# Attention keys with four rows of a column side by side, and one sum of bias and mask for the two middle query tiles

## The chip, the cores and the metric

The kernel runs on one core of one Trainium2 chip. The metric is the time of one execution in microseconds on the device. The kernel before was timed three times: 905.06, 905.87 and 906.93 us, so its median is 905.87 us.

A core has five engines with a queue of instructions each: PE (matrix products; the load of its weights is listed apart as PEld), DVE (vector), ACT (activations), POOL (general) and SP (here only DMA issue). Each engine works its queue in order. [...]

## The reference

One layer over 1024 latent tokens (a grid of 16 rows and 64 columns) and 256 context tokens, width 1024. One input projection feeds two branches, whose outputs are gated, joined and sent through one output projection.

```python
def hybrid_layer(...):
    h = rmsnorm(x, g_pre) * (1.0 + scale[:, None]) + shift[:, None]
    na_q, na_k, na_v, na_z, g_qkv, g_z, g_b, g_a = jnp.split(h @ w_in, IN_SPLITS, axis=-1)
    o_na = neighborhood_attention(heads(na_q), heads(na_k), heads(na_v), heads(na_kc), heads(na_vc), rpb)
    q, k, v = gdn_qkv(g_qkv, conv_w)
    q, k = axial_rope(q, rope), axial_rope(k, rope)
    beta, g = gdn_gates(g_b, g_a, A_log, dt_bias)
    o_g, o_gc = bidirectional_gdn(q, k, v, g, beta, qc, kc, vc, gc, betac)
    o_g = rmsnorm(o_g, gdn_norm_w).reshape(B, L, GDN_W).astype(x.dtype)
    y = jnp.concatenate([o_na * jax.nn.silu(na_z), o_g * jax.nn.silu(g_z)], axis=-1) @ w_out
    x = x + gate[:, None] * rmsnorm(y, g_post)

def neighborhood_attention(q, k, v, k_ctx, v_ctx, rpb):       # row_block, for each grid row r
    rs = jnp.clip(r - kh // 2, 0, rows - kh)                  # kh = 8 rows, NA_KW = 16 columns
    k_win = k_rows[:, :, col_idx]
    bias = rpb[:, row_off[:, None, None], col_off[None, :, :]]
    s_loc = jnp.einsum('bchd,bicjhd->bhcij', q_r, k_win) + bias
    s_ctx = jnp.einsum('bchd,bnhd->bhcn', q_r, k_ctx)
    p = jax.nn.softmax(jnp.concatenate([s_loc, s_ctx], axis=-1), axis=-1)
    return p_loc @ v_win + p_ctx @ v_ctx                      # as einsums

def gated_delta_chunked(...):                                 # chunk by chunk, one direction
    def step(state, xs):
        v_new = u_n - w_n @ state
        o_n = q_n @ state + qk_n @ v_new
        state = state * gl_n + k_n.T @ v_new
```

There are 8 attention heads of 64 and 4 delta heads of 128; the delta scan runs in both directions.

## The kernel before

**Stages.** Projections, convolution and the preparation of the scan take the first 554 us. Then attention and the delta scan run together (`phase_b`), and the output projection (`phase4`) closes the kernel. Instructions are recorded in program order and then put in an order by a scheduler, which works by a model of the engines and of the buffers; on the chip that order is fixed, engine by engine.

**Keys.** `qk_out` takes a projected tile of queries (i = 0) or keys (i = 1) of a pair of heads from PSUM: ACT writes its rounded part `hi` (L522, tile `sh_k` or `sh_q`), DVE the remainder `lo` (L523, `sl_k` or `sl_q`), and two DMAs bring both to `qk_dram`. gr is 0 or 1 for the 512 latents of 8 grid rows, 2 for the 256 context tokens. Keys of latents lie row by row, 64 columns in a row.

**Attention.** `na_attn` loads a pair of heads p (keys `kk`, queries `qh` and `ql`, bias rows `gt`, values `vv`) and runs 2 × 4 units, rt by ct: rt is the half of the grid, ct the tile of query columns. A unit (`na_unit`) treats 128 queries of 8 rows by 16 columns and both heads hh. Its window is three blocks of four rows with NCOLS = 24, 32, 32, 24 columns for ct = 0 to 3, so n = 288 or 384 keys in three runs of m = 96 or 128. For each head:

- POOL adds bias and mask to `gm` (L676). GCOL0 and CTYPE give the part of the bias and the mask; for ct = 1 and 2 they are the same.
- PE multiplies by the context keys into `pc` (L684) and by the window's keys into `pl` (L688), each with `qh` and `ql`. In L688 the keys are read with the four rows of a column after one another, 64 elements apart.
- DVE takes the largest context score `mi` (L692), and adds `gm` to `pl` and takes the common maximum `nm` (L693); ACT takes the exponentials (L694, L695).
- PE transposes the probabilities into the banks of `pl` and `pc` (L697, L702), DVE and ACT copy them to `tl` and `tcx` (L699, L704), and PE multiplies them with the values into `po` (L710, L715).

After four units DVE gathers the sums, POOL spreads their reciprocals to `rb` (L618), PE transposes these (`prt`, L621), and DVE scales the output `zs` (L623). There are two buffers of `gm` and three of the tiles that hold probabilities.

**Scan.** `delta_scan` runs 4 heads with 10 steps, both directions d in a step. POOL scales `kd` and `vb` (L1125, L1128). Per direction PE, DVE, PE, ACT, PE and DVE follow one another: L1133 into `pa`, `y` (L1134), L1138, `vn` (L1140 or L1142), L1144, the new state `s` (L1147). The output products L1152 and L1153 go to `pos`. The head's output is normed (ACT squares at L1170, POOL L166, L167, L1173; L1175 on POOL or L1179 on DVE), transposed (`ot`, L1182) and gated (L1184). 1.40 steps are recorded for each attention unit.

**Output weights.** After the third pair, and again for the rest in `phase4`, `split_w` loads half a block of `w_out` to `wor` (two buffers), ACT rounds it (L647), POOL takes the remainder (L648). `phase4` multiplies by them in three products each (L1218 to L1220), beginning with the attention output of the last pair, which `split_m` casts (L659, L660).

Of the kernel before, what the change touches and what calls it, by code (L numbers as in the profile page):

```python
# [11 lines left out]
F32 = mybir.dt.float32  # L12
F32R = mybir.dt.float32r
I32 = mybir.dt.int32
AF = mybir.ActivationFunctionType
ALU = mybir.AluOpType
# [4 lines left out]
P = 128  # L21
# [9 lines left out]
KCOL0 = (0, 8, 24, 40)  # L31
# [108 lines left out]
class K:  # L140
    def __init__(self, tc, I, out, dbg=None):
        self.tc, self.nc, self.I, self.out = tc, tc.nc, I, out
        self.dbg = dbg or {}
        self.na_first = None
        self.gate = self.after = None

    def order(self, r, before):
# [369 lines left out]
    def qk_out(self, p, i, gr, src):  # L517
        nc = self.nc
        n, scale, c0 = 512 if gr < 2 else CT, 1.0 if i else 0.125, S * i + 512 * gr
        src, rows = src[:, :n], slice(P * p, P * p + P)  # L520
        hi, lo = (self.wp.tile([P, 512], F32R, name=f"s{c}_{'qk'[i]}{p}{gr}", tag="st", bufs=4)[:, :n] for c in "hl")
        nc.scalar.activation(hi, src, AF.Copy, scale=scale)  # L522
        nc.vector.scalar_tensor_tensor(lo, src, scale, hi.bitcast(F32), ALU.mult, ALU.subtract)  # L523
        nc.sync.dma_start(self.qk_dram[0, rows, c0:c0 + n], hi.bitcast(F32))
        nc.sync.dma_start(self.qk_dram[1, rows, c0:c0 + n], lo.bitcast(F32))

# [136 lines left out]
    def na_unit(self, ps, p, rt, ct, qk, vv, gts, mk, sums, po):  # L663

        nc = self.nc
        u = 4 * rt + ct
        nco = NCOLS[ct]
        n, m = 12 * nco, 4 * nco
        mo = MOFF[(rt, CTYPE[ct])]
        tls, tcs = [], []  # L670
        for hh in range(2):
            gt = gts[hh]
            gv = bass.AP(gt.tensor, gt[:, (4 * (1 - rt)) * 31 + GCOL0[ct]:].offset,
                         [list(gt.ap[0]), [4 * 31, 3], [1, nco], [31, 4]])
            gm = self.nw.tile([P, 384], F32, name=f"gm{p}_{u}_{hh}", tag="gm", bufs=2)
            nc.gpsimd.tensor_tensor(gm[:, :n].rearrange("p (n c r) -> p n c r", c=nco, r=4), gv,  # L676
                                    mk[:, mo:mo + n].rearrange("p (n c r) -> p n c r", c=nco, r=4), ALU.add)
            pcb = ps.tile([P, 512], F32, name=f"pc{p}_{u}_{hh}", tag="sc", bufs=2)
            pl = ps.tile([P, 512], F32, name=f"pl{p}_{u}_{hh}", tag="sl", bufs=2)
            pc = pcb[:, :256]  # L680
            pl3 = pl[:, :n].rearrange("p (n c r) -> p n c r", c=nco, r=4)
            qs, kk = qk[hh]
            for i, a in enumerate(qs):
                nc.tensor.matmul(pc, a[:, u * P:(u + 1) * P], kk[:, S:S + CT], start=(i == 0), stop=(i == 1))  # L684
            kv = kk[:, 256 * rt:256 * rt + 768].rearrange("p (n r c) -> p n c r", c=64, r=4)[
                :, :, KCOL0[ct]:KCOL0[ct] + nco, :]
            for i, a in enumerate(qs):
                nc.tensor.matmul(pl3, a[:, u * P:(u + 1) * P], kv, start=(i == 0), stop=(i == 1))  # L688
            mi = self.nw.tile([P, 1], F32, name=f"mi{p}_{u}_{hh}", tag="mi", bufs=4)
            nm = self.nw.tile([P, 1], F32, name=f"nm{p}_{u}_{hh}", tag="nm", bufs=4)  # L690
            pt = self.nw.tile([P, 640], F32, name=f"pt{p}_{u}_{hh}", tag="pt", bufs=3)
            nc.vector.tensor_reduce(mi, pc, AX.X, ALU.max, negate=True)  # L692
            nc.vector.tensor_tensor_reduce(pt[:, :n], pl[:, :n], gm[:, :n], -1.0, mi, ALU.add, ALU.min, nm)  # L693
            nc.scalar.activation(pt[:, :n], pt[:, :n], AF.Exp, bias=nm, scale=-1.0, accum_out=sums[:, ct, hh, 0:1])  # L694
            nc.scalar.activation(pt[:, 384:640], pc, AF.Exp, bias=nm, accum_out=sums[:, ct, hh, 1:2])  # L695
            for rc in range(3):
                nc.tensor.transpose(pl[:m, rc * P:(rc + 1) * P], pt[:, rc * m:(rc + 1) * m], self.ident)  # L697
            tl = self.nw.tile([P, 384], F32, name=f"tl{p}_{u}_{hh}", tag="tl", bufs=4)
            nc.vector.tensor_copy(tl[:m, :], pl[:m, :384])  # L699
            tls.append(tl)  # L700
            for cc in range(2):
                nc.tensor.transpose(pc[:, cc * P:(cc + 1) * P], pt[:, 384 + cc * P:384 + (cc + 1) * P], self.ident)  # L702
            tcx = self.nw.tile([P, 2, P], F32, name=f"tcx{p}_{u}_{hh}", tag="tcx", bufs=4)
            nc.scalar.copy(tcx.rearrange("p c q -> p (c q)"), pc)  # L704
            tcs.append(tcx)

        for cc in range(2):
            for hh in (1, 0):
                hb = 64 * hh
                nc.tensor.matmul(po[hb:hb + 64, ct, :], self.vcx[:, cc, P * p + hb:P * p + hb + 64], tcs[hh][:, cc, :],  # L710
                                 start=(cc == 0), stop=False, tile_position=(0, hb))
        for rc in range(3):
            for hh in (1, 0):
                hb = 64 * hh
                nc.tensor.matmul(po[hb:hb + 64, ct, :], vv[:m, ct, rt + rc, hb:hb + 64], tls[hh][:m, rc * P:(rc + 1) * P],  # L715
                                 start=False, stop=(rc == 2), tile_position=(0, hb))
# [677 lines left out]
```

## Time and profile before

| | |
|---|---|
| Median of three runs | 905.87 us (905.06 to 906.93) |
| Profiled execution | 904.01 us, of which its span is 902.3 us |
| Mean granted clock of PE in it | 0.963 |
| First score product of attention | 554.23 us |
| First weight product of the output projection | 791.59 us |
| Last product, end of the span | 894.89 us, 902.3 us |
| L676, sums of bias and mask | 64: 32 of 128x288 at 891 ns, 32 of 128x384 at 1127 ns |
| L688, window's scores | 128 products; 288 columns with `qh` 409 ns, 384 columns 455 ns |

A row of a timeline has start and duration in us, the engine, the line, the operation with its output and inputs, the number of instructions, and in brackets the engine's idle time before it with what ended it. A row of groups has the count, then the busy time in us and the mean in ns, then the idle time of the engine before them. A row of the windows has for each engine its busy time with the number of instructions, then the granted clock of PE as a share of full speed, the DMA share and GB/s. A busy PE is modelled: its products overlap, so steps from start to start are the better measure.

### The profile page before, as it was taken

How to read it: one execution, taken by the hardware profiler on the slowest of the kernel's cores; microseconds unless marked ns; L12 is line 12 of the kernel's file. 1: busy time of each engine (PE TensorE's matmuls, PEld its weight loads, DVE VectorE, ACT ScalarE, POOL GpSimd, SP SyncE). 2: the span in 40 equal slices, each digit the busy share in tenths (PEclk: the TensorE clock that was granted, in tenths of full speed). 3: DMA queues.
4: the chain of work that ended last, by engine and by line, in shares of the span. 5: the costliest groups of instructions: out<-in, count | busy, mean ns of one | idle time of the engine just before them, and what ended most of it. 6: DMA issues, size and time to landing. Idle time of an engine off the chain costs nothing.

```text
span 902.3 us, 16602 instructions
## 1 busy us (share of the span) xinstructions
PE 848.5 (94%) x6082; PEld 708.7 (79%) x6082; DVE 537.6 (60%) x1179; ACT 416.2 (46%) x1165; POOL 369.6 (41%) x431
## 2 busy tenths in 40 slices
PE   6999999999999989998998998999999988998996
PEld 4688887887788767787887877888887876887785
DVE  3463454456545699689428634677777775662442
ACT  5262525545645445652334444555545656532310
POOL 1432322614543532455241124568557569423210
PEclk9999999999999989999998985999999998999898
DMA  9786432346355534733799699949387152132351
GB/s 343 257 290 228 150 107 74 114 157 199 89 198 185 138 122 151 216 99 112 249 265 265 219 281 413 267 117 296 141 208 272 48 183 76 47 117 94 108 183 60
DMA packets 95176, 160.98 MB, mean 178 GB/s; under 512 B 28581, under 2 KB 55542, under 8 KB 92918
## 3 DMA queue, kind: packets, MB, share of 16 engines
q1 hardware_dynamic: 87606, 146.25, 51.2%
q10 hardware_dynamic: 7488, 13.67, 4.9%
q8 instruction: 48, 0.79, 0.4%
q14 instruction: 34, 0.28, 0.1%
HBM read 110.82 MB, written 52.42 MB: 181 GB/s over the span
## 4 chain that ended last, share of the span: by engine, by line
PE 64%; DVE 13%; DMA 9%; ACT 5%; issue 4%; POOL 2%; SPq 2%; ACTq 0%; DVEq 0%; POOLq 0%
PE py L1218 3%; PE py L1219 3%; PE py L1220 3%; DVE tb L1003 3%; PE pl L688 2%; DVE vb L1006 2%; PE po L715 2%; PE pl L697 2%; PE pz L464 2%; PE pc L684 2%; PE pz L460 2%; PE pz L465 2%; PE po L710 2%; PE pa L1138 2%; PE pa L1144 2%
## 5 line engine op out<-in xcount | busy, mean ns | idle before, releaser
L676 POOL TENSOR_TENSOR gm<-gt,mk 128x288 f32<-128x288 f32 (+1 forms) x64 | 64.3, 1009 | 36.0 <-DVE nm L693 35.9
L1125 POOL TENSOR_SCALAR kd<-kt,kd 128x128 f32<-128x128 f32 x72 | 43.4, 606 | 35.3 <-PE pa L1144 33.7
L694 ACT ACTIVATE pt<-pt,nm 128x288 f32<-128x288 f32 (+1 forms) x64 | 36.7, 574 | 35.7 <-DVE nm L693 35.5
L945 ACT ACTIVATE em<-em,gc 128x128 f32<-128x128 f32 x80 | 25.5, 391 | 38.2 <-DMA em<-gc_dram 32.3
L693 DVE CUSTOM_DVE_ANT_0 pt<-pl,gm,mi 128x288 f32<-128x288 f32 (+1 forms) x64 | 36.1, 564 | 11.5 <-PE pl L688 4.9
L699 DVE COPY tl<-pl 96x384 f32<-96x384 f32 (+1 forms) x64 | 35.3, 551 | 10.2 <-PE pl L697 9.9
L692 DVE TENSOR_REDUCE mi<-pc 128x1 f32<-128x256 f32 x64 | 26.8, 420 | 22.0 <-PE pc L684 21.1
L464 PE MATMUL pz<-hl,wh_gz 128*128 128x512 f32 x96 | 38.6, 402 | 0.0
L460 PE MATMUL pz<-hh,wh_gz 128*128 128x512 f32 x96 | 38.4, 400 | 0.0
L465 PE MATMUL pz<-hh,wl_gz 128*128 128x512 f32 x96 | 38.3, 399 | 0.0
L473 PE MATMUL pv<-wh_nv,hh 128*128 128x264 f32 x128 | 35.5, 295 | 2.5 <-ACT hh L262 1.7
L964 POOL TENSOR_SCALAR_AFFINE_SELECT qe<-qe 128x256 f32<-128x256 f32 x32 | 26.9, 840 | 25.8 <-DVE qe L963 25.8
L475 PE MATMUL pv<-wl_nv,hh 128*128 128x264 f32 x128 | 35.7, 286 | 1.5 <-POOL wl_nv L446 1.5
L474 PE MATMUL pv<-wh_nv,hl 128*128 128x264 f32 x128 | 36.5, 289 | 0.0
L1003 DVE TENSOR_TENSOR tb<-ab,vb 120x31 f32<-120x31 f32 (+15 forms) x62 | 32.1, 518 | 6.8 <-DMA ab<-ab_dram 5.1
L960 DVE SCALAR_TENSOR_TENSOR pm<-pk,beta,em 128x128 f32<-128x128 f32 x80 | 23.6, 343 | 19.9 <-PE pk L953 12.3
L697 PE MATMUL pl<-c,pt 128*96 128x128 f32 (+1 forms) x192 | 33.7, 285 | 1.4 <-ACT pt L694 1.2
L812 DVE SCALAR_TENSOR_TENSOR acc_v<-xp_v,cols,acc_v 128x1282 f32<-128x1282 f32 x16 | 27.5, 1719 | 9.0 <-ACT acc_v L810 8.9
L1138 PE MATMUL pa<-y,tm 128*128 128x128 f32 x144 | 29.1, 287 | 2.8 <-DVE y L1134 2.2
L1266 ACT ACTIVATE finv<-py 128x512 f32<-128x512 f32 x16 | 9.5, 599 | 46.8 <-PE py L1220 28.3
L1128 POOL TENSOR_SCALAR vb<-v,beta 128x128 f32<-128x128 f32 x40 | 24.2, 606 | 16.7 <-DVE y L1134 10.6
L704 ACT COPY tcx<-pc 128x256 f32<-128x256 f32 x64 | 23.8, 372 | 15.3 <-PE pc L702 15.1
(438 smaller groups left out, 2928.8 us busy)
## 6 DMA issues: line engine op xcount, KB each, us to landing
wada<-in_w_ada SPq DMA_DIRECT2D x16, 512.0 KB, 9.1
em<-gc_dram SPq DMA_DIRECT2D x20, 256.0 KB, 4.6
pm_dram<-pm SPq DMA_DIRECT2D x20, 256.0 KB, 3.3
pmf<-pm_dram SPq DMA_DIRECT2D x8, 640.0 KB, 8.0
tm_dram<-tm SPq DMA_DIRECT2D x8, 640.0 KB, 7.0
kk<-qk_dram SPq DMA_DIRECT2D x16, 320.0 KB, 7.9
tm<-tm_dram SPq DMA_DIRECT2D x4, 1280.0 KB
kq_dram<-kq SPq DMA_DIRECT2D x4, 1152.0 KB
```

The source lines that it names most:

```text
L460: r = nc.tensor.matmul(ps, wh, xh, start=(k == 0), stop=False)
L464: nc.tensor.matmul(ps, wh, xl, start=False, stop=False)
L465: nc.tensor.matmul(ps, wl, xh, start=False, stop=(k == KC - 1))
L474: nc.tensor.matmul(ps, xl, wh, start=False, stop=False)
L475: nc.tensor.matmul(ps, xh, wl, start=False, stop=(k == KC - 1))
L676: nc.gpsimd.tensor_tensor(gm[:, :n].rearrange("p (n c r) -> p n c r", c=nco, r=4), gv, mk[:, mo:mo + n].rearrange("p (n c r) -> p n c r", ...
L693: nc.vector.tensor_tensor_reduce(pt[:, :n], pl[:, :n], gm[:, :n], -1.0, mi, ALU.add, ALU.min, nm)
L694: nc.scalar.activation(pt[:, :n], pt[:, :n], AF.Exp, bias=nm, scale=-1.0, accum_out=sums[:, ct, hh, 0:1])
L697: nc.tensor.transpose(pl[:m, rc * P:(rc + 1) * P], pt[:, rc * m:(rc + 1) * m], self.ident)
L1003: nc.vector.tensor_tensor(t3, bc(ab[:, 0:m, m:m + 1], [r, m, n]), bc(vb[:, m:m + 1, m:], [r, m, n]), ALU.mult)
L1125: nc.gpsimd.tensor_scalar(kd, kt_[:, t, :], self.kd[:, h, d, t:t + 1], None, ALU.mult)
L1138: nc.tensor.matmul(pa, tm[:, d, t, :], y, start=True, stop=True)
```

## The change

Three things are edited. Keys of latents are written in `qk_out` with the four rows of a column side by side: ACT and DVE read the PSUM tile in the order block, column, row, and write SBUF contiguously; for keys, whose scale is 1, DVE's fused operation becomes a plain subtraction. L688's moving operand then is three contiguous runs of m elements. And `gm` is made only for ct = 0, 1 and 3; the unit ct = 2 reads the sum that ct = 1 left, for which there are three buffers instead of two.

```diff
+        self.gm = {}
...
-        nc.scalar.activation(hi, src, AF.Copy, scale=scale)
-        nc.vector.scalar_tensor_tensor(lo, src, scale, hi.bitcast(F32), ALU.mult, ALU.subtract)
+
+        kv = lambda v, o: v.rearrange(f"p (n {o}) -> p n c r", r=4, c=64) if i and gr < 2 else v
+        nc.scalar.activation(kv(hi, "c r"), kv(src, "r c"), AF.Copy, scale=scale)
+        if i:
+            nc.vector.tensor_tensor(kv(lo, "c r"), kv(src, "r c"), kv(hi, "c r").bitcast(F32), ALU.subtract)
+        else:
+            nc.vector.scalar_tensor_tensor(lo, src, scale, hi.bitcast(F32), ALU.mult, ALU.subtract)
...
-            gm = self.nw.tile([P, 384], F32, name=f"gm{p}_{u}_{hh}", tag="gm", bufs=2)
-            nc.gpsimd.tensor_tensor(gm[:, :n].rearrange("p (n c r) -> p n c r", c=nco, r=4), gv,
-                                    mk[:, mo:mo + n].rearrange("p (n c r) -> p n c r", c=nco, r=4), ALU.add)
+
+            if ct != 2:
+                self.gm[hh] = self.nw.tile([P, 384], F32, name=f"gm{p}_{u}_{hh}", tag="gm", bufs=3)
+                nc.gpsimd.tensor_tensor(self.gm[hh][:, :n].rearrange("p (n c r) -> p n c r", c=nco, r=4), gv,
+                                        mk[:, mo:mo + n].rearrange("p (n c r) -> p n c r", c=nco, r=4), ALU.add)
+            gm = self.gm[hh]
...
-            pl3 = pl[:, :n].rearrange("p (n c r) -> p n c r", c=nco, r=4)
+            pl3 = pl[:, :n].rearrange("p (n f) -> p n f", f=m)
...
-            kv = kk[:, 256 * rt:256 * rt + 768].rearrange("p (n r c) -> p n c r", c=64, r=4)[
-                :, :, KCOL0[ct]:KCOL0[ct] + nco, :]
+            kv = kk[:, 256 * rt:256 * rt + 768].rearrange("p (n f) -> p n f", f=256)[
+                :, :, 4 * KCOL0[ct]:4 * KCOL0[ct] + m]
```

The added lines shift what follows: L688 becomes L697, L697 becomes L706, L1138 becomes L1147 and so on, by 6 to 9 lines.

The order on the engines is the same up to the start of attention, and differs from there on. In the rows the numbers after a name are its pair or head, then the unit and the head hh, or the direction and the chunk.

PE where attention begins, before: the first two products of the scan stand just ahead of the first unit's transposes.

```order
L1138 MATMUL pa0_0_5883<-v0_5781,tm0_5783 128x128
L1138 MATMUL pa0_1_5884<-vb0_1_1_5896,tm0_5783 128x128
L697 MATMUL pl0_0_0_5725<-c128_60,pt0_0_0_5732 96x128 x3
L702 MATMUL pc0_0_0_5724<-c128_60,pt0_0_0_5732 128x128 x2
L1144 MATMUL pa0_0_5883<-vn0_0_0_5888,kd0_0_0_5886 128x128
L697 MATMUL pl0_0_1_5749<-c128_60,pt0_0_1_5756 96x128 x3
```

PE at the same place in the changed kernel, from the same product on.

```order
L1147 MATMUL pa0_0_5883<-v0_5781,tm0_5783 128x128
L1147 MATMUL pa0_1_5884<-vb0_1_1_5896,tm0_5783 128x128
L1153 MATMUL pa0_0_5883<-vn0_0_0_5888,kd0_0_0_5886 128x128
L1153 MATMUL pa0_1_5884<-vn0_1_1_5898,kd0_1_1_5894 128x128
L1142 MATMUL pa0_0_5883<-s0_0_0_5892,kq0_5780 128x128
L1142 MATMUL pa0_1_5884<-s0_1_1_5902,kq0_5780 128x128
```

The scan goes on here without a unit between: 52 of its products, from L1153 above, stand ahead of the first transposes. This is the end of that piece in the changed kernel.

```order
L1161 MATMUL pos0_5885<-s0_1_7_6130,kq0_5780 128x128
L1162 MATMUL pos0_5885<-vn0_1_6_6231,qe0_5784 128x128
L1147 MATMUL pa0_0_5883<-y0_0_6_6301,tm0_5783 128x128
L1147 MATMUL pa0_1_5884<-y0_1_5_6318,tm0_5783 128x128
L706 MATMUL pl0_0_0_5725<-c128_60,pt0_0_0_5732 96x128 x3
L711 MATMUL pc0_0_0_5724<-c128_60,pt0_0_0_5732 128x128 x2
```

So the scan is about five and a half steps further when the first unit's transposes come. On POOL the first unit's `gm` has moved likewise, from ahead of the scan's first `vb` and `kd` to behind the `kd` of its seventh step.

POOL in the last pair, before, up to `rb` of its first half (names of `wor` and `wo` carry the block of weights).

```order
L648 TENSOR_TENSOR wo_kk15_8317<-wor1_0_8318,wo_kk04_8316 128x512
L1128 TENSOR_SCALAR vb3_1_6_8812<-v3_8387,beta_1271 128x128
L648 TENSOR_TENSOR wo_kk15_8317<-wor1_512_8322,wo_kk04_8316 128x512
L676 TENSOR_TENSOR gm3_4_1_8761<-gt3_1_7609,mk_4989 128x288
L167 TENSOR_TENSOR rq_y_o2_8264<-rq_y_o2_8264,mhalf_67 128x8
L1125 TENSOR_SCALAR kd3_1_7_8705<-kt3_8388,kd_1310 128x128
L1125 TENSOR_SCALAR kd3_0_5_8795<-kt3_8388,kd_1310 128x128
L618 COPY rb3_0_8727<-rs3_0_8723 128x512
L1128 TENSOR_SCALAR vb3_1_5_8844<-v3_8387,beta_1271 128x128
L648 TENSOR_TENSOR wo_tm7_8398<-wor2_0_8399,wo_o6_8397 128x512
```

POOL there in the changed kernel.

```order
L684 TENSOR_TENSOR gm3_4_0_8709<-gt3_0_7591,mk_4989 128x288
L684 TENSOR_TENSOR gm3_4_1_8733<-gt3_1_7593,mk_4989 128x288
L654 TENSOR_TENSOR wo_kk15_8293<-wor1_0_8294,wo_kk04_8292 128x512
L654 TENSOR_TENSOR wo_kk15_8293<-wor1_512_8298,wo_kk04_8292 128x512
L684 TENSOR_TENSOR gm3_5_0_8831<-gt3_0_7591,mk_4989 128x384
L654 TENSOR_TENSOR wo_tm7_8374<-wor2_0_8375,wo_o6_8373 128x512
L654 TENSOR_TENSOR wo_tm7_8374<-wor2_512_8379,wo_o6_8373 128x512
L624 COPY rb3_0_8699<-rs3_0_8695 128x512
L1134 TENSOR_SCALAR kd3_0_6_8799<-kt3_8364,kd_1310 128x128
```

The scan's `kd` and `vb` have left this place, and two more splits of `w_out` stand ahead of `rb`: eight instead of six.

PE behind the last transposes of attention, before.

```order
L621 MATMUL prt3_1_9126<-c128_60,rb3_1_9124 128x128 x4
L1133 MATMUL pa3_1_8408<-s3_1_5_8853,kq3_8386 128x128
L1152 MATMUL pos3_8409<-s3_1_7_8716,kq3_8386 128x128
L1153 MATMUL pos3_8409<-vn3_1_6_8817,qe3_8390 128x128
L1144 MATMUL pa3_0_8407<-vn3_0_7_8922,kd3_0_7_8917 128x128
L1138 MATMUL pa3_1_8408<-y3_1_4_8936,tm3_8389 128x128
```

PE there in the changed kernel.

```order
L627 MATMUL prt3_1_9094<-c128_60,rb3_1_9092 128x128 x4
L1161 MATMUL pos3_8385<-s3_0_8_8984,kq3_8362 128x128
L1162 MATMUL pos3_8385<-vn3_0_9_9068,qe3_8366 128x128
L1161 MATMUL pos3_8385<-s3_1_3_9001,kq3_8362 128x128
L1162 MATMUL pos3_8385<-vn3_1_2_9080,qe3_8366 128x128
L1227 MATMUL py0_0_9166<-wo_qh00_8272,m3_9100 128x512
```

Before, 32 products of the scan follow here, mixed with weight products, and both groups of its output's transposes (L1182) stand behind 147 of the 384 weight products. After, the four shown remain, and the groups stand behind 105 and 128 weight products.

## The prediction

> **What bounds the kernel now.** I read the page's first part, then the windows of the attention stage, then the timeline of PE.
>
> ```profile
> PE 848.5 (94%) x6082; PEld 708.7 (79%) x6082; DVE 537.6 (60%) x1179; ACT 416.2 (46%) x1165; POOL 369.6 (41%) x431
> 557.00:640.00 83.00, 79.41 (x701) 69.37 (x700) 59.50 (x188) 46.28 (x174) 53.99 (x73) 0.98 0.85 251
> 720.00:790.00 70.00, 63.22 (x537) 53.81 (x538) 46.22 (x142) 39.02 (x137) 45.92 (x56) 0.95 0.29 99
> 740.00:760.00 20.00, 17.02 (x143) 13.70 (x144) 12.01 (x36) 14.24 (x55) 19.55 (x24) 1.00 0.36 124
> 540.00:557.00 17.00, 13.28 (x212) 12.61 (x210) 6.64 (x16) 5.77 (x14) 5.12 (x8) 0.50 1.02 417
> ```
>
> PE is the bound: 79.4 of 83 us at the start of attention, with POOL at 54.0. Only in the last pair is POOL fuller than PE (19.55 against 17.02 of 20 us). So an edit pays by what it takes from PE or from PE's waits. The stage is cut by its eight reciprocal transposes, which close each half pair (four units):
>
> ```profile
> 554.23 0.58 PE L684 MATMUL pc<-kk,qh 128*128 128x256 f32 x1
> 585.17 0.60 PE L621 MATMUL prt<-c,rb 128*128 128x128 f32 x4
> 612.75 0.60 PE L621 MATMUL prt<-c,rb 128*128 128x128 f32 x4
> 640.64 0.60 PE L621 MATMUL prt<-c,rb 128*128 128x128 f32 x4
> 669.01 0.60 PE L621 MATMUL prt<-c,rb 128*128 128x128 f32 x4
> 697.79 0.60 PE L621 MATMUL prt<-c,rb 128*128 128x128 f32 x4
> 728.88 0.60 PE L621 MATMUL prt<-c,rb 128*128 128x128 f32 x4
> 759.76 0.66 PE L621 MATMUL prt<-c,rb 128*128 128x128 f32 x4 [1.32 <-POOL rb L618]
> 788.89 0.60 PE L621 MATMUL prt<-c,rb 128*128 128x128 f32 x4
> 894.89 0.40 PE L1220 MATMUL py<-wl,mh 128*128 128x512 f32 x1
> ```
>
> Stretches: 30.9 us to the first, then 27.6, 27.9, 28.4, 28.8, 31.1, 30.9, 29.1, and 106.0 to the last matmul.
>
> **Scores.** A matmul's cost on PE is the step from its start to the next start.
>
> ```profile
> 564.85 0.28 PE L684 MATMUL pc<-kk,ql 128*128 128x256 f32 x1
> 564.97 0.38 PE L1144 MATMUL pa<-vn,kd 128*128 128x128 f32 x2
> 565.39 0.37 PE L688 MATMUL pl<-kk,ql 128*128 128x384 f32 x1
> 565.60 0.38 PE L1133 MATMUL pa<-s,kq 128*128 128x128 f32 x2
> ```
>
> 256 contiguous columns take 0.12 us, 384 strided ones 0.21. At the contiguous rate 384 columns would take 0.18, so contiguous keys save about 0.03 us on the `ql` product; the `qh` product's step is blurred by the weight load before it. 64 × 0.03 = 1.9 us if `qh` gains nothing, twice that if it gains as much, nothing if the saving is only the pattern's three runs: **−2 us** (0 to −4).
>
> **Evictions.** ACT and DVE now read the eight 512-column key tiles from PSUM out of order.
>
> ```profile
> L522 ACT ACTIVATE sh_k<-pk x12: 374/582/600, 67.8 to 511.0; 128x512 fp32r<-128x512 f32 x8, 128x256 fp32r<-128x256 f32 x4
> L523 DVE SCALAR_TENSOR_TENSOR sl_k<-pk,sh_k x12: 410/680/693, 71.7 to 511.7; 128x512 fp32r<-128x512 f32 x8, 128x256 fp32r<-128x256 f32 x4
> L1267 DVE TENSOR_TENSOR finv<-py,ggb x16: 681/691/693, 846.9 to 896.0; 128x512 f32<-128x512 f32 x16
> L623 DVE TENSOR_TENSOR zs<-prt,zs x8: 680/686/692, 586.0 to 789.5; 128x512 f32<-128x512 f32 x8
> ```
>
> The plain subtraction from PSUM (L1267, 691 ns) costs what the fused one does (680). L623 reads PSUM in strided runs of 16 at 686 ns. No row shows single elements 64 apart; if they doubled the time, 8 × 0.58 + 8 × 0.68 = 10 us of ACT and DVE, beside PE's projection products and on their way to DRAM long before 554 us. Taken: **0**, by the nearest row, L623 (0 to +2, where PE waits for the bank; a gain has no source).
>
> The Trainium skill, "Advanced Engine Details and Errata" (Memory Cachelines, PSUM), speaks against this edit: in PSUM every two elements in a row should be contiguous for best throughput. By it the reads would pay, and the sum would be up to 2 us higher. L623, whose runs are longer than two, cannot decide it, and no row here shows shorter ones.
>
> **Bias sums.** 16 of these on 128x384 go:
>
> ```profile
> L676 POOL TENSOR_TENSOR gm<-gt,mk 128x384 f32<-128x384 f32 x32 | 35.9, 1127 | 21.5 <-DVE nm L693 21.5
> ```
>
> 16 × 1.127 = 18.0 us of POOL. The row's idle time says that POOL waits 21.5 us for DVE to release the old sum. No instruction waits for `gm` in the view of waits. By itself this is worth **0** in pairs 0 to 2 (down to −2 from units that start sooner); the last pair is below.
>
> **The order.** The third buffer lets the recorder move the scan ahead. Fp32 products of the scan cost 0.222 us each (two instructions; 789.59 to 789.82 below). I counted them in PE's two orders, for the opening, the seven stretches and the tail. Before: 46, 47, 27, 48, 34, 54, 34, 30, 32. After: 93, 32, 54, 28, 56, 32, 7, 46, 4.
>
> ```profile
> 789.59 0.39 PE L1152 MATMUL pos<-s,kq 128*128 128x128 f32 x2
> 789.82 0.39 PE L1153 MATMUL pos<-vn,qe 128*128 128x128 f32 x2
> L1134 DVE SCALAR_TENSOR_TENSOR y<-pa,nsc,vb 128x128 f32<-128x128 f32 x36 | 12.4, 344 | 1.8 <-PE pa L1133 1.7
> L1140 ACT ACTIVATE vn<-pa,beta 128x128 f32<-128x128 f32 x40 | 14.6, 365 | 13.6 <-PE pa L1138 12.4 <-PE pos L1153 1.0
> L1147 DVE SCALAR_TENSOR_TENSOR s<-s,egl,pa 128x128 f32<-128x128 f32 x64 | 21.8, 341 | 3.9 <-PE pa L1144 3.4
> ```
>
> *Opening.* 52 scan products now stand in one piece before the first `pl` transpose. A scan step is a chain: L1133 0.39, y 0.34, L1138 0.39, vn 0.37, L1144 0.39, s 0.34 (products as at 789.59), with some 0.05 at each of six hand-overs: 2.5 us, and two directions share DVE, so I take 2.8 to 3.1 against PE's 10 × 0.222 = 2.2. Five steps waste 3 to 4.5 us; the first links and the late `gm` before the transposes add about 2. Less about 1 for gaps that stand there today, that is +5.2 idle and 47 × 0.222 = +10.4 of work taken from later: **+15.6**, of which the idle is +3 to +10.
>
> *Pairs 0 to 2.* Less their scan products, the five stretches before last 17.1, 21.9, 17.7, 21.3 and 19.1 us: about 17.4 for four units, 21.6 where a head's output transposes (L1182) lie in it. After: 28.7, 29.4, 27.8, 29.8, 28.7 = 144.4 against 143.8: **+0.6**.
>
> On SP's queue the next scan head's loads now stand ahead of the next pair's:
>
> ```profile
> 567.18 0.45 SPq L153 DMA_DIRECT2D kk<-qk_dram  x1
> ```
>
> The pair that is loaded from here is first used behind 612.75; 45 us hide the move: 0.
>
> *Last pair, first half.* Only seven scan products fill it, so PE's own work is 17.4 + 1.6 = 19 us. But `rb` now stands on POOL behind eight splits of the output weights instead of six.
>
> ```profile
> 734.53 0.43 SPq L153 DMA_DIRECT2D wor<-in_w_out  x1
> 739.57 1.28 POOL L648 TENSOR_TENSOR wo_ql<-wor,wo_qh 128x512 fp32r<-128x512 f32 x1 [2.70 <-ACT wo_qh L647]
> 740.88 0.33 SPq L153 DMA_DIRECT2D wor<-in_w_out  x1
> 744.30 0.60 ACT L647 CAST wo_qh<-wor 128x512 fp32r<-128x512 f32 x1
> 759.09 0.62 POOL L618 COPY rb<-rs 128x512 f32<-128x512 f32 x1
> ```
>
> The first split starts 10.7 us after the transposes at 728.88. A raw buffer freed at 740.85 is reloaded at 740.88, cast from 744.30 to 744.90, and can then be split: 5.4 us a round, two buffers. The fourth round starts at 10.7 + 3 × 5.4 = 26.9 and ends 3 us later, so `rb` comes 30 us after 728.88, where it stands today (30.2). Behind the waiting transposes PE's whole queue stands still, the next units' scores first. The loads set this, not POOL's work, so the lighter POOL does not help. The stretch stays at **30.9** (±0), PE idle for up to 10 us in it. *Second half:* 17.4 + 46 × 0.222 = 27.6: **−1.5**.
>
> *Clock.* An idle of several us halves the clock: the tail shows it.
>
> ```profile
> 831.80:837.20 5.40, 1.71 (x10) 0.84 (x9) 2.80 (x4) 0.76 (x2) 1.61 (x3) 0.92 0.08 31
> 837.79 0.63 PE L1219 MATMUL py<-wo_qh,m 128*128 128x512 f32 x1
> 838.22 0.63 PE L1220 MATMUL py<-wo_ql,m 128*128 128x512 f32 x1
> 826.00:843.00 17.00, 12.83 (x48) 9.61 (x47) 5.82 (x8) 6.35 (x21) 7.22 (x7) 0.80 0.33 117
> ```
>
> After 3.7 us idle of 5.4, a product's step is 0.43 us. The last pair ran at a mean clock of 0.95 already; a longer idle adds **+1.3** (0 to +3).
>
>
> *Tail.* Before, 32 scan products (7.1 us) and the last head's transposes follow the last `prt`, with 3.7 us idle around the transposes and about 3 lost at half clock. After, four scan products remain and the transposes lie among weight products. 106.0 − 28 × 0.222 − 6.7, plus about 1 for a wait ahead of the first product (its cast of the attention output follows the last `prt`, with less scan to cover it): **−11.9** (−14 to −6).
>
> **Sum.** 15.6 + 0.6 + 0 − 1.5 + 1.3 − 11.9 = +4.1; less 2 for the scores and evictions at 0: **+2.1** on the profiled run's 904.0, which is 906.1. The median of the runs shown (905.87) lies 1.9 us above that run, so 908.0.
>
> **Rivals.** *Faster: the last pair does not wait.* If `rb` came with PE's own work, near 24 us (casts run earlier on an idle ACT, rounds of 4 us), its stretch gives −7 and the clock term goes: 908.0 − 8.3 = 899.7. For it: POOL at 19.55 of 20 us was the limit there and loses its sums and scan scalings. Against it: 740.88 to 744.30 is load time, which nothing shortens. *Slower: the scan alone never wakes the clock.* Attention began at clock 0.50. If the opening runs at half clock for 13 us longer than before, some 6.5 us of work are added: 914.5. It decides if PE's waits in the chain count as idle. For it: 0.50 from 540 to 557 with PE at 13.28 of 17. Against it: at half clock a step's 2.2 us of work becomes 4.4, which the chain no longer starves. The Trainium skill, "TensorE: Matmul & The Clock Gate" (Part 1), has a rule against it too: some 3.4 us of sustained work restore the full clock. By an estimate from it this rival would cost about 2 us instead of 6.5; the window at 0.50 for 17 us shows that such a spell can be far longer here. *The layout does nothing:* strided keys were free, and PSUM reads out of order cost 1 us: 911.0.
>
> **How the numbers follow.** Forecast 0.36, faster rival 0.36, half clock 0.18, layout 0.10. The range 898.5 to 916 reaches from the faster rival to the slower one, with the idle bounds of the opening. A measurement can tell 0.2% here, 1.8 us: faster is below 904.1, slower above 907.7. Forecast (±2.5 us): 0.01, 0.15, 0.20; faster rival 0.30, 0.05, 0.01; half clock 0, 0, 0.18; layout 0, 0.03, 0.07. Sums: faster 0.31, same 0.23, slower 0.46.
>
> **What would show it.** L688's steps at 0.18 us; `sh_k` and `sl_k` unchanged; the first `prt` 46.5 us after the first `pc`; the seventh again about 31 us after the sixth, with PE idle for `rb` and a clock below 1; nothing idle between the last weight products. A seventh stretch below 25 us, or an opening above 50, makes it wrong.

## The result and the profile after

The changed kernel takes 912.82 us in the median of six runs (910.95 to 914.69), the kernel before 905.54 (902.32 to 906.93): the ratio is 1.0083, 95% interval 1.0061 to 1.0105. It is slower by 7.3 us. The forecast was 908.0 us, slower by 2.1.

The first part of the page of the changed kernel, busy time by engine:

```profile
PE 852.0 (93%) x6082; PEld 711.7 (78%) x6082; DVE 535.3 (59%) x1179; ACT 418.1 (46%) x1165; POOL 353.6 (39%) x415
```

The group of the larger sums, by form:

```profile
L684 POOL TENSOR_TENSOR gm<-gt,mk 128x384 f32<-128x384 f32 x16 | 18.0, 1127 | 19.2 <-DVE nm L702 19.2
```

The two evictions of keys, line by line (shortest, median and longest in ns):

```profile
L525 ACT ACTIVATE sh_k<-pk x12: 384/581/600, 69.0 to 516.1; 128x512 fp32r<-128x512 f32 x8, 128x256 fp32r<-128x256 f32 x4
L527 DVE TENSOR_TENSOR sl_k<-pk,sh_k x12: 412/680/692, 72.7 to 516.7; 128x512 fp32r<-128x512 f32 x8, 128x256 fp32r<-128x256 f32 x4
```

Then the window in which the tail's idle time lay before, in the changed kernel, and the whole tail, of the changed kernel and of the kernel before:

```profile
831.80:837.20 5.40, 5.40 (x25) 4.36 (x24) 0.87 (x1) 1.05 (x1) 0.34 (x1) 1.00 0.46 146
811.70:904.80 93.10, 92.00 (x405) 74.13 (x404) 38.57 (x57) 24.99 (x60) 19.81 (x25) 1.00 0.39 130
788.90:895.00 106.10, 101.83 (x462) 82.60 (x460) 43.33 (x78) 26.57 (x68) 21.62 (x28) 0.97 0.34 115
```

POOL's busy time fell from 369.6 to 353.6 us, as 16 sums went. The evictions of the keys (the copies out of PSUM, the memory that PE writes its products to) cost what they did: 581 and 680 ns in the middle, against 582 and 680. The window that held 3.7 us of idle PE before is full, at full clock. The tail begins at another time in the two kernels, so its whole is the better comparison: PE stood idle 1.1 us in it instead of 4.3, at a clock of 1.00 instead of 0.97.

The product of the keys with `ql` on 384 columns now steps on after 0.18 us, where it took 0.21; after the one with `qh` the step is 0.28 us here as it was before:

```profile
787.84 0.44 PE L697 MATMUL pl<-kk,qh 128*128 128x384 f32 x1
788.12 0.34 PE L697 MATMUL pl<-kk,ql 128*128 128x384 f32 x1
788.30 0.38 PE L711 MATMUL pc<-c,pt 128*128 128x128 f32 x2
```

The stage is cut as in the prediction. These rows of the timeline are the changed kernel's first score product, its eight reciprocal transposes and its last product:

```profile
559.21 0.58 PE L693 MATMUL pc<-kk,qh 128*128 128x256 f32 x1
606.11 0.60 PE L627 MATMUL prt<-c,rb 128*128 128x128 f32 x4
633.47 0.60 PE L627 MATMUL prt<-c,rb 128*128 128x128 f32 x4
663.84 0.60 PE L627 MATMUL prt<-c,rb 128*128 128x128 f32 x4
689.45 0.60 PE L627 MATMUL prt<-c,rb 128*128 128x128 f32 x4
719.14 0.60 PE L627 MATMUL prt<-c,rb 128*128 128x128 f32 x4
749.12 0.60 PE L627 MATMUL prt<-c,rb 128*128 128x128 f32 x4
783.77 0.60 PE L627 MATMUL prt<-c,rb 128*128 128x128 f32 x4
811.71 0.60 PE L627 MATMUL prt<-c,rb 128*128 128x128 f32 x4
904.82 0.40 PE L1229 MATMUL py<-wl,mh 128*128 128x512 f32 x1
```

Their differences, beside those of before and of the forecast, in us:

| | opening | five stretches of pairs 0 to 2 | seventh | eighth | tail | sum |
|---|---|---|---|---|---|---|
| before | 30.9 | 143.7 | 30.9 | 29.1 | 106.0 | 340.7 |
| forecast, ahead of the layout and clock terms | 46.5 | 144.4 | 30.9 | 27.6 | 94.1 | 343.5 |
| after | 46.9 | 143.0 | 34.7 | 27.9 | 93.1 | 345.6 |

From the first score on, the changed kernel loses 4.9 us; 5.0 more lie ahead of it, where attention starts at 559.2 instead of 554.2 us. That is 9.9 us between these two executions, where the medians differ by 7.3. The seventh stretch is the one that missed. PE's, ACT's, POOL's and SP's rows of the timeline in it, of the changed kernel:

```profile
762.02 0.75 PE L706 MATMUL pl<-c,pt 128*128 128x128 f32 x3 [3.97 <-ACT pt L703]
769.55 0.55 PE L706 MATMUL pl<-c,pt 128*128 128x128 f32 x3 [1.79 <-ACT pt L703]
777.01 0.80 PE L1161 MATMUL pos<-s,kq 128*128 128x128 f32 x2 [3.28 <-DVE o L1169]
...
760.74 0.62 ACT L653 CAST wo_qh<-wor 128x512 fp32r<-128x512 f32 x1 [3.38 <-DMA wor<-in_w_out]
761.27 0.61 ACT L703 ACTIVATE pt<-pt,nm 128x384 f32<-128x384 f32 x1
...
775.75 0.62 ACT L653 CAST wo_o<-wor 128x512 fp32r<-128x512 f32 x1 [2.96 <-DMA wor<-in_w_out]
776.27 0.36 ACT L1165 ACTIVATE o<-pos,egc 128x128 f32<-128x128 f32 x1
...
771.51 2.64 POOL L654 TENSOR_TENSOR wo_kk<-wor,wo_kk 128x512 fp32r<-128x512 f32 x2 [0.47 <-ACT wo_kk L653]
...
779.40 0.61 POOL L624 COPY rb<-rs 128x512 f32<-128x512 f32 x1
...
756.31 0.32 SPq L154 DMA_DIRECT2D zs<-z_dram  x1
756.68 0.42 SPq L154 DMA_DIRECT2D wor<-in_w_out  x1
772.81 1.69 SPq L154 DMA_DIRECT2D wor<-in_w_out  x2
```

The window over it, then its last part ahead of the transposes, then the same stretch of the kernel before:

```profile
749.00:784.00 35.00, 23.92 (x176) 18.86 (x175) 15.43 (x43) 18.20 (x55) 16.91 (x16) 0.85 0.43 136
777.00:782.40 5.40, 5.39 (x29) 4.85 (x31) 1.93 (x7) 3.53 (x12) 3.11 (x4) 0.50 0.29 99
728.90:759.80 30.90, 26.70 (x227) 22.16 (x225) 20.83 (x65) 19.90 (x73) 25.50 (x31) 1.00 0.49 169
```

PE's longest idle, 3.97 us, ends with an exponential that ACT begins at 761.27. ACT itself had waited 3.38 us for a load of output weights, since a cast of them stands ahead of that exponential in its queue. At 775.75 another cast waits 2.96 us, and behind it the scan's output (776.27), for which PE's next product waits by way of DVE. The first of these loads comes no sooner because it stands behind the load of `zs` at 756.31. The one for 775.75 comes no sooner because its buffer is free only when the first of POOL's splits from 771.51 has ended: it is issued at 772.81. `rb` comes at 779.40, 30.3 us after the transposes at 749.12, and PE reaches its transposes only at 783.77. From 777.0 on it does not wait at all, but works at half clock up to 782.4: what holds it back are the waits for ACT and the clock, not `rb`. Over the whole stretch PE is idle for 11 of 35 us at a granted clock of 0.85; before, it was idle for 4 of 31 at 1.00.

### The profile page after: what moved, and what is told of

The parts are those of the page before. It is cut to its first block, busy times and chain, and to the rows that moved or that the text cites. A ratio compares the mean times of both kernels' runs of the same rounds, so it can differ in the third digit from the quotient of the medians.

```text
span 912.2 us, 16609 instructions
## 1 busy us (share of the span) xinstructions
PE 852.0 (93%) x6082; PEld 711.7 (78%) x6082; DVE 535.3 (59%) x1179; ACT 418.1 (46%) x1165; POOL 353.6 (39%) x415
## 5 line engine op out<-in xcount | busy, mean ns | idle before, releaser
L684 POOL TENSOR_TENSOR gm<-gt,mk 128x288 f32<-128x288 f32 (+1 forms) x48 | 46.4, 973 | 25.8 <-DVE nm L702 25.6
L703 ACT ACTIVATE pt<-pt,nm 128x288 f32<-128x288 f32 (+1 forms) x64 | 36.7, 574 | 33.4 <-DVE nm L702 32.6
L701 DVE TENSOR_REDUCE mi<-pc 128x1 f32<-128x256 f32 x64 | 26.7, 420 | 29.5 <-PE pc L693 29.1
L706 PE MATMUL pl<-c,pt 128*96 128x128 f32 (+1 forms) x192 | 33.1, 283 | 7.6 <-ACT pt L703 7.3
L969 DVE SCALAR_TENSOR_TENSOR pm<-pk,beta,em 128x128 f32<-128x128 f32 x80 | 23.5, 343 | 22.4 <-PE pk L962 12.9
L1153 PE MATMUL pa<-vn,kd 128*128 128x128 f32 x144 | 29.8, 292 | 2.4 <-POOL vb L1137 1.1
L1142 PE MATMUL pa<-s,kq 128*128 128x128 f32 x144 | 29.8, 291 | 2.2 <-DVE s L1156 1.9
```

Source lines behind the costliest of these rows:

```text
L684: nc.gpsimd.tensor_tensor(self.gm[hh][:, :n].rearrange("p (n c r) -> p n c r", c=nco, r=4), gv, mk[:, mo:mo + n].rearrange("p (n c r) -> p ...
L1142: nc.tensor.matmul(pa, kt, st[d], start=True, stop=True)
L1153: nc.tensor.matmul(pa, kd, vn, start=True, stop=True)
```

## The experiments

**Theory.** The third buffer of `gm` makes the loss, through the order it lets the scheduler make: the scan runs alone in the opening, and the last pair lacks scan products to cover ACT's waits for weight loads. The covered tail gives part of it back; the layout is a small gain. **Rivals.** The out-of-order PSUM reads delay the stages ahead; sharing the sum itself costs; the rounds of splits ahead of `rb` set the last pair; the opening runs at half clock.

In all runs the stretches are worked out as above, from the same ten starts on PE.

**e1, the layout alone.** The edits of `qk_out` and L688 on the kernel before, the two buffers and the 64 sums as they were:

```diff
+        kv = lambda v, o: v.rearrange(f"p (n {o}) -> p n c r", r=4, c=64) if i and gr < 2 else v
+        nc.scalar.activation(kv(hi, "c r"), kv(src, "r c"), AF.Copy, scale=scale)
...
+            kv = kk[:, 256 * rt:256 * rt + 768].rearrange("p (n f) -> p n f", f=256)[
+                :, :, 4 * KCOL0[ct]:4 * KCOL0[ct] + m]
```

> The key layout alone, with two buffers of gm and 64 sums; every engine keeps the order of before (scan products by stretch 46, 47, 27, 48, 34, 54, 34, 30, 32). Theory A (the order makes the loss, the layout saves a little): attention's first score product near 554 us as before, the stretches as before less 0.4 us each, the whole 2 to 4 us faster than before, ratio 0.996 to 0.998. Theory B (the out-of-order PSUM reads of the keys make the 5 us by which attention began later in the changed kernel's profile): first score product near 559 us, the whole 1 to 3 us slower than before.

Measured: 902.72 us against 903.48, ratio 0.9987 (0.9970 to 1.0004), so no change that this measurement can tell. From first score to last product 337.1 us instead of 340.7 (339.3 in e7): every stretch of pairs 0 to 2 is 0.3 to 0.5 us shorter. Attention began at 556.25, between what the two theories said. The whole gained 0.8 us where 2 to 4 were expected; why the gain of the stretches does not show in it stays open. The rows of groups of the four products in e1:

```profile
L694 PE MATMUL pl<-kk,qh 128*128 128x384 f32 x32 | 13.3, 415 | 0.3 <-DVE tl L705 0.2
L694 PE MATMUL pl<-kk,qh 128*128 128x288 f32 x32 | 12.3, 384 | 1.3 <-DVE zs L629 0.8 <-DVE tl L705 0.4
L694 PE MATMUL pl<-kk,ql 128*128 128x384 f32 x32 | 10.8, 338 | 0.0
L694 PE MATMUL pl<-kk,ql 128*128 128x288 f32 x32 | 9.8, 305 | 0.0
```

Before, they lasted 455, 409, 383 and 334 ns, so each is 25 to 45 ns shorter.

**e2, the shared sum with three buffers alone.**

```diff
+            if ct != 2:
+                self.gm[hh] = self.nw.tile([P, 384], F32, name=f"gm{p}_{u}_{hh}", tag="gm", bufs=3)
...
+            gm = self.gm[hh]
```

> The shared sum with three buffers alone, keys row by row as before; PE's order is that of the changed kernel (93, 32, 54, 28, 56, 32, 7, 46, 4 scan products by stretch). Theory A: first score product near 554 us or wherever a run happens to put it, opening stretch 46 to 47 us, the seventh stretch 33 to 36, the tail 93 to 94, and the whole 8 to 11 us slower than before, 2 to 4 slower than the changed kernel. Theory B: 3 to 6 us slower than before, as the eviction's cost is gone.

Measured: 914.05 us, ratio 1.0097 (1.0072 to 1.0123). Opening 46.8, seventh stretch 36.7 (33 to 36 expected), tail 93.1, sum 347.9. The loss is there without any new PSUM read.

**e3, both edits with two buffers.**

```diff
-                self.gm[hh] = self.nw.tile([P, 384], F32, name=f"gm{p}_{u}_{hh}", tag="gm", bufs=3)
+                self.gm[hh] = self.nw.tile([P, 384], F32, name=f"gm{p}_{u}_{hh}", tag="gm", bufs=2)
```

> Both edits, with two buffers of gm instead of three: the opening stays as before (46 scan products), the last pair's first half keeps 24 of them, the tail has 9. Theory A (the opening's waits and the last pair's waits make the loss, the covered tail is a gain): opening 31 us, seventh stretch 30 to 34, tail 94 to 96, the whole 6 to 12 us faster than before. Rival (the tail's gain needs the scan to be ahead from the start, or the sharing itself costs): within 2 us of before.

Measured: 897.48 us, ratio 0.9909 (0.9882 to 0.9936): faster by 6.0 us than the kernel before timed beside it, by 14 than the changed kernel (e4). Opening 29.8, seventh stretch 34.8, tail 94.7, sum 331.8. The opening's loss is gone and the tail's gain stays, so the latter did not need the scan to run ahead from the start. The opening is 17 us shorter than in the changed kernel, and putting its 47 scan products back among the later units costs only some 3. The seventh stretch did not fall to the 30 to 34 us expected: with 24 scan products in it, it is as long as the changed kernel's with seven. The products do cover waits, as PE is idle for 5.8 us there instead of 11, but the lack of them is not what makes the stretch long, and this part of the theory fell.

**e4, the changed kernel again.** No edit.

> The changed kernel as it is, for a second profile beside the others. If the late start of attention (559 us) is a matter of one execution, its first score product comes between 554 and 557 us here; if it belongs to the change, again near 559. Stretches as in the first profile within 1 us: 46.9, 27.4, 30.4, 25.6, 29.7, 30.0, 34.7, 27.9, 93.1.

Measured: 911.63 us, ratio 1.0083 (1.0053 to 1.0113). First score at 561.0, opening 46.3, seventh stretch 37.1, the other stretches within 1.3 us of the first profile, sum 346.1. The late start was there again. This profile, at 916.23 us, is 4.6 us above the median of its runs. The window over its seventh stretch:

```profile
749.00:786.10 37.10, 26.01 (x173) 20.76 (x172) 15.35 (x43) 18.04 (x55) 16.89 (x16) 0.77 0.44 138
```

PE is idle for 11 us here too, so the 2.4 us more than in the first profile go with the lower clock, 0.77 against 0.85.

**e5 and e6, weight loads not held back.** In the changed kernel (e5) and in e3 (e6), `split_w` no longer orders its loads behind the last load of `zs`; the scheduler then sends the first of them ahead of it, and makes another order of the scan as well (98 scan products in the opening and 21 in the seventh stretch of e5, against 93 and 7):

```diff
-            self.load(raw, self.I["w_out"][k * P:(k + 1) * P, o:o + 512], self.na_last)
+            self.load(raw, self.I["w_out"][k * P:(k + 1) * P, o:o + 512])
```

> The changed kernel, but the loads of the output weights (wor) no longer stand behind the last load of zs; scan products by stretch are 98, 37, 51, 27, 54, 26, 21, 38, 0. Theory A (in the last pair ACT's casts of the weights stand ahead of exponentials and wait for these loads, and PE waits for the exponentials): no wait of several us on ACT for wor, the seventh stretch 22 to 26 us instead of 34.6 to 37.1, the opening still 46 to 49, from the first score to the last product 330 to 335 us instead of 345.6 to 346.1. Rival (the rounds of the splits ahead of rb set the stretch, whenever the loads come): seventh stretch 30 or more, the sum 339 or more.

> The same freeing of the weight loads in the version with both edits and two buffers (its seventh stretch took 34.8 us); scan products 46, 47, 37, 53, 35, 56, 18, 54, 6. Theory A: seventh stretch 25 to 27 us, the sum 322 to 327 instead of 331.8, the whole 13 to 18 us faster than before. Rival: seventh stretch 31 or more, the sum 329 or more.

e5: 904.34 us, ratio 0.9999 (0.9979 to 1.0019), so the whole loss is gone. Opening 49.1, seventh stretch 30.2, sum 338.8. The seventh stretch fell by 4.5 to 6.9 us, but to the rival's 30, not to 22 to 26. Rows of e5's timeline in it show why (ACT, PE, POOL, PE):

```profile
755.09 0.62 ACT L653 CAST wo_kk<-wor 128x512 fp32r<-128x512 f32 x1 [3.96 <-DMA wor<-in_w_out]
756.37 0.90 PE L706 MATMUL pl<-c,pt 128*128 128x128 f32 x3 [3.28 <-ACT pt L703]
774.27 0.61 POOL L624 COPY rb<-rs 128x512 f32<-128x512 f32 x1
776.25 0.60 PE L627 MATMUL prt<-c,rb 128*128 128x128 f32 x4
```

The window around the first two:

```profile
754.00:762.00 8.00, 4.94 (x23) 3.82 (x23) 2.61 (x7) 5.28 (x16) 3.81 (x4) 0.57 0.61 204
```

One cast, of the third block of weights, still waits 3.96 us, PE waits 3.28 behind it, and the clock stands at 0.57 for 8 us. Again PE comes later than `rb`. So a cast still holds PE up behind a load, as the theory has it, though by its length the stretch fits the rival's forecast: one of the waits had stayed. The sixth to eighth stretches together fell from 92.6 and 93.7 us to 81.4 with the same 85 scan products in them; opening and tail took back some 4. As the scan was spread anew by the same edit, e5 alone does not tell the loads from the order.

e6: 893.53 us, ratio 0.9883 (0.9864 to 0.9902), the fastest kernel of all, though 13 to 18 us were expected and 11.1 came. Seventh stretch 27.1, sum 327.1. The third buffer costs here as well: e5 is 10.8 us slower. The row of the window over the seventh stretch of e6, and its `rb`:

```profile
735.00:762.00 27.00, 22.86 (x201) 18.72 (x201) 17.40 (x50) 17.08 (x65) 18.91 (x24) 1.00 0.46 159
760.56 0.61 POOL L624 COPY rb<-rs 128x512 f32<-128x512 f32 x1 [1.87 <-DVE rs L621]
```

Here no cast waits longer than 1.5 us for a load, PE's longest wait is 1.27 us, and the clock is 1.00. `rb` waits for DVE, so the rounds of splits do not set the stretch here. The sixth and the eighth grew by 2.5 and 1.9 us against e3, so the three together gained 3.4 and not 7.7.

**e7, the kernel before again.** No edit.

> The kernel before, for a second profile. If the part ahead of attention, whose order no variant changes, only wanders from execution to execution, its first score product comes anywhere from 554 to 561 us, as it did in the six profiles so far; if the changed evictions or the larger pool delay it, again within 1 us of 554.2. Stretches as in the first profile: 30.9, 27.6, 27.9, 28.4, 28.8, 31.1, 30.9, 29.1, 106.0.

Measured: 906.15 us in its one run. First score at 557.75, sum 339.3. So the part ahead wanders by 3.5 us in the kernel before, too.

**e8, the third buffer alone.** One digit of the kernel before:

```diff
-            gm = self.nw.tile([P, 384], F32, name=f"gm{p}_{u}_{hh}", tag="gm", bufs=2)
+            gm = self.nw.tile([P, 384], F32, name=f"gm{p}_{u}_{hh}", tag="gm", bufs=3)
```

> Only the third buffer of gm; 64 sums and the old key layout. Scan products 93, 40, 51, 37, 51, 23, 7, 44, 6. Theory A (the buffer's order makes the loss): opening 46 to 48 us, seventh stretch 34 to 38, tail 93 to 94.5, the whole 7 to 12 us slower than before. Rival (the loss comes from sharing the sum, which makes ct = 2 wait for the sum of ct = 1): opening as before, within 2 us of before.

Measured: 917.38 us, ratio 1.0148 (1.0125 to 1.0170). Opening 46.6, seventh stretch 36.5, tail 93.6, sum 350.9. A buffer more, and nothing else in the program as it is written, makes the kernel 13 us slower, a little beyond the 7 to 12 expected.

**e9, the shared sum with two buffers, and e10, free weight loads in the kernel before.** e9 is e2 with `bufs=2`; e10 is the kernel before with the edit of e5.

> The shared sum with two buffers and the old key layout; its order is that of e3_both_two_buffers (46, 47, 37, 53, 35, 53, 24, 48, 9). If the layout is worth the 3.6 us that e1_keys_only showed between first score and last product, the sum is 335 to 336 us (e3: 331.8), the stretches each 0.3 to 0.5 us longer than e3's, and the whole 3 to 7 us faster than before. If the layout's saving is swallowed by waits in this order, the sum is within 1 us of 331.8.

> The kernel before, with the weight loads no longer held behind the last load of zs; scan products 46, 47, 27, 48, 34, 57, 31, 46, 16. Theory A (waits of casts on these loads cost the last pair some 5 us in the kernel before as well): seventh stretch 24 to 27 us instead of 30.8, the tail 100 to 103, the sum 331 to 335 instead of 339.3 to 340.7, the whole 5 to 9 us faster. Rival (the freed loads help only where the lighter POOL or the shifted scan leaves room, as in e6): seventh stretch 29 or more, the whole within 3 us of before.

e9: 899.22 us, ratio 0.9920 (0.9900 to 0.9940), sum 333.7, 1.9 more than e3. So sharing the sum does not cost: alone, with two buffers, it is 6.4 us faster. The layout is worth 1.9 us in this order, some 2 us in the order of three buffers (347.9 in e2 against 345.6 and 346.1), and 2.2 to 3.5 in the old one. e10: 897.90 us, ratio 0.9916 (0.9889 to 0.9944). Seventh stretch 28.4, tail 95.7, sum 330.1: better than expected, though the seventh stretch kept a wait of 1.97 us. But the gain does not lie in that stretch: the sixth to eighth together take 91.2 us, against 91.1 and 90.6 before, now with 134 scan products instead of 118. The sum falls by 9.2 to 10.6 us because the tail falls by 10, and the tail has 16 scan products left instead of 32. So a new order came with the freed loads here too, and how much the loads themselves cost the kernel before is not shown.

## Why the prediction came out as it did

The sign was right, with 0.46 on slower, and the time lay inside the range; the mechanism of the opening and of the tail was right too. The size was not: 7.3 us slower instead of 2.1, outside the 2.5 us set around the forecast. The time stands between the 911.0 and the 914.5 us of two rivals whose mechanisms both fell, so that the range held it is in part luck. By its steps:

- **Opening, forecast +15.6:** measured +16.0 and +15.4. e8 shows that the third buffer alone makes it (46.6), e3 that it goes with that buffer (29.8). A step of the scan alone took somewhat more than the 2.8 to 3.1 us put down for it: the starts of three successive steps' groups of L1147, in the changed kernel's timeline,

```profile
567.63 1.00 PE L1147 MATMUL pa<-y,tm 128*128 128x128 f32 x4
570.84 0.72 PE L1147 MATMUL pa<-y,tm 128*128 128x128 f32 x4
574.18 0.72 PE L1147 MATMUL pa<-y,tm 128*128 128x128 f32 x4
```

  lie 3.2 and 3.3 us apart.
- **Half clock in the opening (the slower rival):** fell. The windows of the changed kernel there, and one of the kernel before, show the clock back within the piece, though PE had gaps:

```profile
560.00:565.00 5.00, 4.68 (x21) 3.98 (x19) 1.19 (x4) 0.63 (x2) 1.79 (x3) 0.57 1.00 415
565.00:570.00 5.00, 4.37 (x26) 3.21 (x25) 1.99 (x7) 1.52 (x5) 3.11 (x6) 1.00 1.02 420
557.00:560.00 3.00, 3.00 (x15) 2.58 (x14) 1.73 (x5) 2.40 (x11) 3.00 (x4) 0.53 0.98 400
```

  If the clock is either 1.00 or 0.50, as in the windows that lie wholly in one of them, a mean of 0.57 is half clock for 4.3 of the 5 us: up to 564.3, some 5.1 us behind the first score product. Before, 0.53 up to 560 gives half clock up to 559.8, some 5.6 us behind it. So the opening got no more half clock than it had.
- **Pairs 0 to 2, forecast +0.6:** measured −0.7 and −2.0, into which the layout's saving falls.
- **Seventh stretch, forecast 30.9 with the clock term of +1.3 beside it:** measured 34.7 and 37.1. This is the step that failed, in the wait and in the clock. The wait: `rb` came when the prediction put it (30.3 us after the last transposes, 30 forecast), but it was not what PE waited for. The prediction read the rounds of the splits on POOL and overlooked that the first half of each round, the cast, sits in ACT's queue ahead of the exponentials. The timeline of before showed such a wait already:

```profile
738.88 1.14 ACT L647 CAST wo_qh<-wor 128x512 fp32r<-128x512 f32 x2 [2.02 <-DMA wor<-in_w_out]
```

  PE's longest wait in that stretch of the kernel before was 1.3 us. In the changed kernel it was 4.0, in e3 and e9, with 24 scan products, 2.4 and 2.7. e5, e6 and e10 take part of the loads' delay away, and the stretch falls by 4.5 to 7.8 us in e5 and e6 and by some 2.5 in e10; with the order changed by the same edit, this is strong but not clean evidence.

  The clock: the forecast allowed up to 10 us of idle PE in the stretch, and 11 came, in both profiles. What was mis-sized is the clock term, +1.3 (0 to +3). By an estimate from the rows above, at most 0.15 × 35 = 5.2 us went to it in the first profile and 0.23 × 37.1 = 8.5 in the second. Taken off, that leaves 29.5 and 28.6 us, so all that lies above 30.9 fits into this term. The twelve profiles bear this out: six have a clock of 0.77 to 0.87 in the stretch, and it takes 34.5 to 37.1 us; five have 1.00, and it takes 27.1 to 30.9; e5 has 0.89 and 30.2.
- **The faster rival** (no wait in the last pair) named the right place; the changed kernel did not show it, and e5 and e6 came part of the way, to 30.2 and 27.1 us instead of 24.
- **Eighth stretch, forecast 27.6, and tail, −11.9:** 27.9, and −12.9.
- **Layout, forecast −2:** 1.8 to 3.5 us from the first score on, by e1, e2 against both profiles of the changed kernel, and e9 against e3, with the step of 0.18 us that was forecast. **Evictions, 0:** their durations did not change, so the up to 2 us that the prediction set beside its sum for reads out of order were not paid there. So the rival that the layout does nothing fell.
- **Sum from the first score on:** the forecast said +2.1, the two profiles of the changed kernel +4.9 against the first profile of before, +6.8 for e4 against e7. The seventh stretch is most of the difference: 2.5 of 2.8 us in the first, all of it in the second.
- **Ahead of the first score** the prediction had no term. All twelve profiles have one order of PE there and began attention anywhere from 554.2 to 561.0 us, the two profiles of the kernel before at 554.2 and 557.75, the two of the changed kernel at 559.2 and 561.0. Whether some of this belongs to the change, and so to the 7.3 us, stays open: e3 and e1, with the same evictions, began at 556.9 and 556.25. Over all, the six profiles with the new evictions began at 558.4 us in the mean (556.25 to 561.0), the six with the old ones at 556.4 (554.2 to 558.2). With so much overlap this does not show a cost, but it does not rule out one of some 2 us ahead of attention, which would eat the layout's saving: in e1 the whole gained 0.8 us.

## What to carry to other kernels

Where a scheduler makes the order, a buffer is part of the program: one buffer more moved half a head of the scan ahead of the attention that it used to fill, and made a change slower that is 6 us faster without it. Before an edit is judged, its order should be compared with and without each such side effect. When work is split between two engines, look at both queues for what stands behind the half that waits for a load. And when a wait of several us is forecast, the work behind it at half clock belongs in the sum: in the seventh stretch the mean clock fell to 0.85 and 0.77.

## What was not expected of the hardware

The stages ahead of attention, with the same instructions in the same order, took from 554.2 to 561.0 us in twelve profiles. A difference of a few us in single profiles is therefore better read from a later common point than from the start of the span. A changed source pattern in PSUM, single fp32 elements 256 bytes apart, cost ACT and DVE nothing that can be seen (581 and 680 ns).
